# v's last additions by accumulating stores, and the recurrence's late passes placed behind the low parts of weights

## The chip, the cores and the metric

The kernel runs on one core of a Trainium2 chip. The metric is the device time of one execution in microseconds (us); of several executions the median is given. One execution is taken by the hardware profiler, and its trace has the start and the duration of the instructions of each engine: PE (TensorE) with its weight loads, DVE (VectorE), ACT (ScalarE), POOL (GpSimd), and SP, which only issues DMAs.

## The reference, cut to what matters

One layer of a streaming encoder, 512 positions by 1024 channels, in float32. A normalised input h goes through one wide projection; its columns feed a pooling mixer, a gated linear recurrence (RG-LRU), a stick-breaking attention with 8 heads, and three gates. The three branches are merged, projected and added to x, and a gated feed-forward follows. What the change touches:

```
proj = einsum('bsd,dc->bsc', h, w_in)          # q, k, v are 1024 columns each
...
a = exp(log_a);  mult = sqrt(-expm1(2 * log_a));  b = mult * (i * xc)
h_t = a_t * h_{t-1} + b_t                      # the recurrence, a scan over positions
...
out = einsum('bhqk,bkhd->bqhd', w, vb)         # attention reads v
```

## The kernel before, in words

Matrix products run in a split form: a float32 operand is written as a high part (rounded to the type fp32r) plus a low part (the rest), and three matmuls (high-high, high-low, low-high) take the place of one. For weights `split_w` (L134 to L143) does it: ScalarE makes the high part `whi` (L141), VectorE subtracts it for the low part `wlo` (L142). High and low parts have three buffers each, so a part can be made only when TensorE is done with the piece three before. Both are traced with a raised priority; the list `los` keeps the low parts' instructions in order.

v, k and q, in this order (`VKQ`), are computed by a Strassen-like scheme of 7 products in place of 8. The unit's weights are four blocks 11, 12, 21, 22, the inputs are quarters of h and sums of them (T1 to T4). The products come in the order 11, 12, S2, S1, S3, S4, 22 (`ORDER`). Each is cut in two pieces of 12 matmuls, i = 0 and 1; in the texts "12,0" is the first piece of product 12. A unit has 14 pieces, 168 matmuls. The sums of weights are made on the way (`add_seven`, L202 to L225): S1 is 21 + 22 by an accumulating load from POOL's queue (L200), S2 is 21 + 22 + 11 on VectorE (tile `qs`, L214), S3 is 11 + 21 by another accumulating load onto 11 (L215), S4 is 12 + S2 on VectorE (L209). For all units the sum qs and the load of L215 follow directly the split of 11. Three pieces' parts are made ahead of the products (`weights`); at the end of some pieces the loads of the next unit's blocks are issued from SP (L198).

The results accumulate in PSUM, in tiles of 128 x 1024. For each quarter (i, j) of the unit's output, ScalarE copies a snapshot of the accumulator into SBUF (`snap`, L857); some products later `final` (L865) adds the rest, read from PSUM, on VectorE. For v the sum is then stored to DRAM from POOL's queue (`store`, L790), for k and q squares, scaling and a transpose come first. v is read again much later, by the attention.

The recurrence runs beside this, in four chunks of 256 channels (c = 0 to 3): ScalarE makes tanh, exp (L695) and a square root (L698), VectorE two decay passes (`lru_decay`, L703 and L705; for chunks 2 and 3 the second is an affine pass of ScalarE, L707), two input passes (`lru_input`, L711 and L712) and two scans (L717). `lru_store` casts the result on ScalarE (L722), takes the low part on VectorE (L723), and stores both from POOL's queue (L725). These passes are put into a background list (`step`, `bg`) and taken from it, one or two at a time, by `tick` calls between pieces. The late passes of chunks 2 and 3 come while v is computed.

The order of the instructions on each engine is fixed when the program is built, by a planner with its own estimates of time: it takes the ready instruction with the highest priority. `tc.high_priority(n)` raises it. `tc.issue_after(ins)` makes an instruction come not before `ins` on its engine; it doesn't say how soon after. At run time each engine works strictly in its fixed order and waits on semaphores.

Of the kernel before, what the change touches and what calls it, by code (L numbers as in the profile page):

```python
# [64 lines left out]
def layer_kernel(ctx: ExitStack, tc: tile.TileContext, x, xt, vecs, w_in, w_qkv7, w_gate7, w_pool, w_rg, w_ig,  # L65
# [125 lines left out]
    def seven_load(n, nms):  # L191
# [3 lines left out]
        for nm in nms:  # L195
            for i in range(pieces):
                qraw[u, nm, i] = r = b4(list(shape), f"qw{u}{nm}{i}", "w")
                nc.sync.dma_start(r, seven_src(u, nm, i))  # L198
                if nm == "21":
                    nc.gpsimd.dma_start(r, seven_src(u, "22", i), accum_op=ALU.add)  # L200

    def add_seven(un, nm, i):  # L202
        u, pieces, shape = UNITS[un]
        last = i == pieces - 1

        def make(n):
            if nm == "S4":
                r = qraw[u, "12", i]
                dve.tensor_tensor(r, r, qraw[u, "S2", i], ALU.add)  # L209
            src = qraw[u, {"S1": "21", "S3": "11", "S4": "12"}.get(nm, nm), i]  # L210
            parts = split_w(src, [P] + list(shape), n)
            if nm == "11":
                qraw[u, "S2", i] = r = b4(list(shape), f"qs{u}{i}")
                dve.tensor_tensor(r, qraw[u, "21", i], src, ALU.add)  # L214
                add = nc.gpsimd.dma_start(src, seven_src(u, "21", i), accum_op=ALU.add)  # L215
            if last:
                if un < 3:
                    seven_load(un + 1, {"S1": ("21",), "S3": ("11",), "S4": ("12",), "22": ("22",)}.get(nm, ()))
                elif un == 3 and nm == "11":
                    with tc.issue_after(add.ins):  # L220
                        seven_load(un + 1, ("21", "11"))
                elif un == 3:
                    seven_load(un + 1, {"12": ("12",), "S2": ("22",)}.get(nm, ()))
            return parts
        specs.append((("seven", u, nm, i), make))  # L225
# [211 lines left out]
    with ExitStack() as first:  # L437
# [263 lines left out]
        def lru_decay(c):  # L701
            e, t = lru[c]["r"], lru[c]["t"]
            dve.scalar_tensor_tensor(t, e, 1.0, t, ALU.add, ALU.mult)  # L703
            if c < 2:
                dve.tensor_scalar(t, t, -1.0, 1.0, ALU.mult, ALU.add)  # L705
            else:
                act(t, t, AF.Identity, scale=-1.0, bias=1.0)  # L707

# [10 lines left out]
        def lru_store(c):  # L719
            y = lru.pop(c)["i"]  # L720
            h, l = b4([2, S], f"yh{c}", "b", F32R), y.bitcast(F32R)
            act(h, y, AF.Copy)  # L722
            dve.tensor_tensor(l, y, h.bitcast(F32), ALU.subtract)  # L723
# [36 lines left out]
        def of(f, c):  # L760
            return lambda: f(c)
# [17 lines left out]
        gate1(2)  # L779
        for f, c in ((lru_decay, 2), (lru_decay, 3), (lru_input, 2)):  # L780
            step(of(f, c))
# [11 lines left out]
        def post(t, i, j, r):  # L793
            if t == 2:
                store(t, i, j, r)
                return
            z = b4([2, 512], f"sq{t}{i}{j}")
# [51 lines left out]
        for t in VKQ:  # L849
# [4 lines left out]
            def snap(key, src):  # L854
                r[key] = b4([2, 512], f"r{t}{key[0]}{key[1]}")
                with tc.high_priority(EARLY):
                    state["snap"] = act(two(r[key]), in_order(src), AF.Copy, scale=-1.0 if key[0] else 1.0)  # L857

            def post_behind(key):
                with tc.issue_after(state["snap"].ins):  # L860
                    post(t, *key, r[key])

            def final(key, src):
                v = two(r[key])
                dve.tensor_tensor(v, v, in_order(src), ALU.subtract if key[0] else ALU.add)  # L865
# [9 lines left out]
            for nm in ORDER:  # L875
# [19 lines left out]
                else:  # L895
                    final((1, 0), ps["22"])
                if (t, nm) == (VKQ[0], "S3"):
                    def last_scan():
                        for j in range(2):
                            with tc.issue_after(los[j - 5]):  # L900
                                lru_scan(3, j)

                    step(of(lru_input, 3)), step(of(lru_scan, 2)), step(last_scan)
                    step(of(lru_store, 2)), step(of(lru_store, 3))
# [899 lines left out]
```

## Time and profile before

| what | value |
|---|---|
| median of 3 runs | 860.64 us (859.68 to 860.79) |
| the profiled execution's own time | 858.89 us |
| its span, first to last instruction | 856.8 us |
| PE busy | 850.3 us (99%) |
| DVE busy | 732.3 us (85%) |
| ACT busy | 533.3 us (62%) |
| POOL busy | 88.6 us (10%) |
| DMA, mean over the span | 180 GB/s |

Busy times of engines overlap. A matmul of 512 columns shows 0.38 us in its row, but the next one starts 0.216 us after it, since they are pipelined; so a loss of TensorE is read from the distance of starts and not from busy time. In a row of the timeline stand the start, the duration, the engine, the line, the operation, the tile written, the tiles read, their sizes, the count, and in brackets the idle time of the engine just before, with what ended it. In rows of groups, the busy time and the mean duration in ns stand behind the bar.

### The profile page before, as it was taken

To read this page: it belongs to the slowest core of one execution; us is meant where nothing else is said; L and a number is where in the kernel's file an instruction comes from. 1 tells how busy PE (TensorE), PEld (TensorE's weight loads), DVE (VectorE), ACT (ScalarE), POOL (GpSimd) and SP (SyncE) were. 2 spreads that over 40 slices of the span, in tenths; PEclk is the share of its full clock that TensorE was granted. 3 is DMA by queue.
4 is the path that set the end of the run, shared out by engine and by line. 5 is a ranking of instruction groups with operands and counts; after the bars stand their busy time and mean duration, and the time that the engine had idled before them with its cause. 6 is when DMAs were issued, how large, how long until landed. Compare 5 with 4: busy or idle time off the path is not lost.

```text
span 856.8 us, 14307 instructions
## 1 busy us (share of the span) xinstructions
PE 850.3 (99%) x5483; PEld 781.2 (91%) x5483; DVE 732.3 (85%) x937; ACT 533.3 (62%) x863; POOL 88.6 (10%) x128
## 2 busy tenths in 40 slices
PE   9999999999999999999999999999999999999998
PEld 7888888888889988889889988889999999999998
DVE  7899898987897699967997877799988888999974
ACT  6554999658887657556665544455655555755642
POOL 1110002123324102000001100000000000121200
PEclk9999999999999999999999999999999999999999
DMA  9586356798585768846668854364533434797913
GB/s 343 160 286 205 101 167 200 215 316 262 141 257 129 228 170 239 246 116 171 174 204 212 182 197 148 99 164 136 145 99 109 114 101 142 221 238 204 199 32 123
DMA packets 141988, 154.09 MB, mean 180 GB/s; under 512 B 41696, under 2 KB 115424, under 8 KB 141920
## 3 DMA queue, kind: packets, MB, share of 16 engines
q1 hardware_dynamic: 129248, 107.30, 40.6%
q0 software_dynamic: 12528, 45.62, 22.5%
q8 instruction: 43, 0.70, 0.3%
q10 hardware_dynamic: 144, 0.26, 0.1%
q14 instruction: 25, 0.20, 0.1%
HBM read 132.71 MB, written 18.87 MB: 177 GB/s over the span
## 4 chain that ended last, share of the span: by engine, by line
PE 88%; ACT 4%; DVE 4%; issue 3%; POOL 1%; DMA 0%; DVEq 0%; POOLq 0%
PE ps_y L315 11%; PE ps_x L315 8%; PE ps_dy L1723 6%; PE ps_q L844 5%; PE ps_dx L1723 5%; PE ps_br L306 3%; PE ps_br L307 3%; PE ps_br L308 3%; PE ps_bY L1347 3%; PE ps_gy L315 3%; PE ps_gate L736 2%; PE ps_bX L1347 2%; PE ps_gx L315 2%; PE ps_pool L308 2%; PE ps_pool L306 2%
## 5 line engine op out<-in xcount | busy, mean ns | idle before, releaser
L141 ACT ACTIVATE whi<-raw 128x1024 fp32r<-128x1024 f32 x69 | 72.9, 1056 | 75.6 <-PE ps_br L307 18.4
L142 DVE TENSOR_TENSOR wlo<-raw,whi 128x1024 fp32r<-128x1024 f32 x69 | 84.2, 1220 | 22.4 <-ACT whi L141 21.9
L142 DVE TENSOR_TENSOR wlo<-qw,whi 128x1024 fp32r<-128x1024 f32 x48 | 58.3, 1220 | 11.6 <-ACT whi L141 11.2
L141 ACT ACTIVATE whi<-qw 128x1024 fp32r<-128x1024 f32 x48 | 50.4, 1052 | 23.6 <-PE ps_q L844 12.8
L1508 ACT ACTIVATE wh_S<-w_S 128x1024 fp32r<-128x1024 f32 x36 | 38.3, 1063 | 28.7 <-PE ps_y L315 20.0
L1629 POOL DMA_DIRECT2D dw<-in_w_down_dram x20 | 17.0, 855 | 305.3 <-DMA dw<-in_w_down_dram 247.7
L1509 DVE TENSOR_TENSOR wl_S<-w_S,wh_S 128x1024 fp32r<-128x1024 f32 x36 | 43.8, 1220 | 3.3 <-ACT wh_S L1508 3.3
L1508 ACT ACTIVATE wh<-w 128x1024 fp32r<-128x1024 f32 x27 | 28.6, 1061 | 28.0 <-PE ps_x L315 9.4
L1509 DVE TENSOR_TENSOR wl<-w,wh 128x1024 fp32r<-128x1024 f32 x27 | 32.9, 1220 | 8.2 <-ACT wh L1508 8.2
L1508 ACT ACTIVATE whdS<-dw 128x1024 fp32r<-128x1024 f32 x20 | 21.2, 1061 | 20.7 <-PE ps_dy L1723 10.6
L1155 DVE TENSOR_TENSOR_SCAN E<-K,ahead 128x512 f32<-128x512 f32 (+3 forms) x32 | 25.4, 814 | 4.6 <-ACT K L1151 4.6
L1509 DVE TENSOR_TENSOR wldS<-dw,whdS 128x1024 fp32r<-128x1024 f32 x20 | 24.3, 1221 | 5.2 <-ACT whdS L1508 5.2
L306 PE MATMUL ps_lru<-HH,whi 128*128 128x512 f32 x64 | 24.6, 384 | 0.0
L306 PE MATMUL ps_br<-yph,whi 128*128 128x512 f32 x64 | 24.4, 382 | 0.0
L306 PE MATMUL ps_gate<-HH,whi 128*128 128x512 f32 x64 | 24.4, 381 | 0.0
L307 PE MATMUL ps_br<-ypl,whi 128*128 128x512 f32 x64 | 24.3, 380 | 0.0
L306 PE MATMUL ps_pool<-HH,whi 128*128 128x512 f32 x64 | 24.3, 379 | 0.0
L306 PE MATMUL ps_br<-yHH,whi 128*128 128x512 f32 x64 | 24.3, 379 | 0.0
L307 PE MATMUL ps_lru<-HL,whi 128*128 128x512 f32 x64 | 24.3, 379 | 0.0
L308 PE MATMUL ps_lru<-HH,wlo 128*128 128x512 f32 x64 | 24.3, 379 | 0.0
L307 PE MATMUL ps_gate<-HL,whi 128*128 128x512 f32 x64 | 24.3, 379 | 0.0
L308 PE MATMUL ps_gate<-HH,wlo 128*128 128x512 f32 x64 | 24.3, 379 | 0.0
(742 smaller groups left out, 3432.1 us busy)
## 6 DMA issues: line engine op xcount, KB each, us to landing
raw<-in_w_in_dram SPq DMA_DIRECT2D x31, 512.0 KB, 5.1
qw<-in_w_qkv_dram SPq DMA_DIRECT2D x24, 512.0 KB, 7.2
dw<-in_w_down_dram POOLq DMA_DIRECT2D x20, 512.0 KB, 7.7
w<-in_w_ffn_gate_dram SPq DMA_DIRECT2D x36, 256.0 KB, 3.9
w<-in_w_ffn_up_dram SPq DMA_DIRECT2D x36, 256.0 KB, 4.1
raw<-in_w_branch_dram SPq DMA_DIRECT2D x16, 512.0 KB, 3.8
qw<-in_w_qkv_dram POOLq DMA_DIRECT2D x12, 512.0 KB, 7.6
g<-gd SPq DMA_DIRECT2D x24, 256.0 KB, 4.5
```

The costliest lines, as they stand in the source:

```text
L141: act(hi, raw, AF.Copy)
L142: los.append(dve.tensor_tensor(lo, raw, hi.bitcast(F32), ALU.subtract).ins)
L306: nc.tensor.matmul(ps, lh, rh, start=start, stop=False, skip_group_check=skip)
L307: nc.tensor.matmul(ps, lh, rl, start=False, stop=False, skip_group_check=skip)
L308: nc.tensor.matmul(ps, ll, rh, start=False, stop=stop, skip_group_check=skip)
L315: nc.tensor.matmul(o, a_[a][:, w, k, :], il2(b_[b][:, k, :]), start=first and n == k == 0, stop=last and n == 2 and k == 3, skip_group_che ...
L844: nc.tensor.matmul(ps[:, a, :], b_[:, k, ts_], il(a_[:, kk, :]), start=first and n == k == 0, stop=n == 2 and k == 3, skip_group_check=True)
L1155: dve.tensor_tensor_scan(E[:, c0:c0 + n][:, ::-1], K[:, c0 + 1:c0 + n + 1][:, ::-1], ahead[:, S - n:][:, ::-1], 0.0, ALU.mult, ALU.add)
L1347: nc.tensor.matmul(o, ah[x_][:, w, k, :], il2(b[k][y_]), start=first_ and n == k == 0, stop=n == 2 and k == 3, skip_group_check=True)
L1508: act(h, src, AF.Copy)
L1509: dve.tensor_tensor(l, src, h.bitcast(F32), ALU.subtract)
L1723: nc.tensor.matmul(o, a_[a][:, w, k0 + k, :], il2(b_[b][:, k, :]), start=first and i == k == 0, stop=last and i == 2 and k == nk - 1, skip ...
```

## The change

Four things:

1. For v, `final` no longer adds on VectorE. The snapshot is stored to DRAM at once; later ScalarE copies the rest out of PSUM into a new SBUF tile, and an accumulating store from POOL's queue adds it to what is in DRAM (`add_store`).
2. For v's unit (un == 0) the sum qs and the accumulating load onto 11 come after the low part of the same piece of 12 and no longer after 11; the sum S4 comes after the low part of the same piece of S2.
3. The late passes of chunks 2 and 3 leave the background list: lru_input 2 and 3 are placed behind the low parts of 12,0 and 12,1, the scans of chunk 2 behind those of S2,0 and S2,1, the scans of chunk 3 behind those of S1,0 and S1,1. Before, lru_input 2 was a step of its own ahead of v, and lru_input 3 and the scans were steps after v's S3.
4. The second decay pass of chunks 2 and 3 goes from ScalarE to VectorE, and so does the cast in `lru_store` for chunks 0 and 1.

```diff
@@ -199,6 +199,8 @@
                 if nm == "21":
                     nc.gpsimd.dma_start(r, seven_src(u, "22", i), accum_op=ALU.add)
 
+    seven_lo = {}
+
     def add_seven(un, nm, i):
         u, pieces, shape = UNITS[un]
         last = i == pieces - 1
@@ -206,13 +208,18 @@
         def make(n):
             if nm == "S4":
                 r = qraw[u, "12", i]
-                dve.tensor_tensor(r, r, qraw[u, "S2", i], ALU.add)
+                with tc.issue_after(seven_lo["S2", i]) if un == 0 else nullcontext():
+                    dve.tensor_tensor(r, r, qraw[u, "S2", i], ALU.add)
             src = qraw[u, {"S1": "21", "S3": "11", "S4": "12"}.get(nm, nm), i]
             parts = split_w(src, [P] + list(shape), n)
-            if nm == "11":
+            if un == 0:
+                seven_lo[nm, i] = los[-1]
+            if nm == ("12" if un == 0 else "11"):
+                first_ = qraw[u, "11", i]
                 qraw[u, "S2", i] = r = b4(list(shape), f"qs{u}{i}")
-                dve.tensor_tensor(r, qraw[u, "21", i], src, ALU.add)
-                add = nc.gpsimd.dma_start(src, seven_src(u, "21", i), accum_op=ALU.add)
+                with tc.issue_after(los[-1]) if un == 0 else nullcontext():
+                    dve.tensor_tensor(r, qraw[u, "21", i], first_, ALU.add)
+                add = nc.gpsimd.dma_start(first_, seven_src(u, "21", i), accum_op=ALU.add)
             if last:
                 if un < 3:
                     seven_load(un + 1, {"S1": ("21",), "S3": ("11",), "S4": ("12",), "22": ("22",)}.get(nm, ()))
@@ -701,10 +708,7 @@
         def lru_decay(c):
             e, t = lru[c]["r"], lru[c]["t"]
             dve.scalar_tensor_tensor(t, e, 1.0, t, ALU.add, ALU.mult)
-            if c < 2:
-                dve.tensor_scalar(t, t, -1.0, 1.0, ALU.mult, ALU.add)
-            else:
-                act(t, t, AF.Identity, scale=-1.0, bias=1.0)
+            dve.tensor_scalar(t, t, -1.0, 1.0, ALU.mult, ALU.add)
 
         def lru_input(c):
             e, s_ = lru[c]["r"], lru[c]["s"]
@@ -719,7 +723,10 @@
         def lru_store(c):
             y = lru.pop(c)["i"]
             h, l = b4([2, S], f"yh{c}", "b", F32R), y.bitcast(F32R)
-            act(h, y, AF.Copy)
+            if c < 2:
+                dve.tensor_copy(h, y)
+            else:
+                act(h, y, AF.Copy)
             dve.tensor_tensor(l, y, h.bitcast(F32), ALU.subtract)
             for d, t in zip(yd, (h, l)):
                 nc.gpsimd.dma_start(d[c // 2][:, 2 * (c % 2):2 * (c % 2) + 2, :], t)
@@ -777,7 +784,7 @@
         gate1(1)
         step(of(lru_scan, 1)), step(g3, of(lru_store, 0)), step(t3, of(lru_store, 1)), step(of(lru_exp, (2, 3)))
         gate1(2)
-        for f, c in ((lru_decay, 2), (lru_decay, 3), (lru_input, 2)):
+        for f, c in ((lru_decay, 2), (lru_decay, 3)):
             step(of(f, c))
         bg.extend(prepare_t())
         gate1(3)
@@ -791,9 +798,6 @@
 
 
         def post(t, i, j, r):
-            if t == 2:
-                store(t, i, j, r)
-                return
             z = b4([2, 512], f"sq{t}{i}{j}")
             sums = qss[:, 2 * j:2 * j + 2, 4 * i:4 * i + 4] if t == 0 else cst.tile(
                 [P, 2, 4], F32, tag="ssq", name=f"ssq{t}{i}{j}", bufs=2)
@@ -855,12 +859,23 @@
                 r[key] = b4([2, 512], f"r{t}{key[0]}{key[1]}")
                 with tc.high_priority(EARLY):
                     state["snap"] = act(two(r[key]), in_order(src), AF.Copy, scale=-1.0 if key[0] else 1.0)
+                if t == 2:
+                    store(t, *key, r[key])
 
             def post_behind(key):
                 with tc.issue_after(state["snap"].ins):
                     post(t, *key, r[key])
 
+            def add_store(key, src):
+                part = b4([2, 512], f"v{key[0]}{key[1]}")
+                with tc.high_priority(EARLY):
+                    act(two(part), in_order(src), AF.Copy, scale=-1.0 if key[0] else 1.0)
+                nc.gpsimd.dma_start(rows(t, *key), part, accum_op=ALU.add)
+
             def final(key, src):
+                if t == 2:
+                    add_store(key, src)
+                    return
                 v = two(r[key])
                 dve.tensor_tensor(v, v, in_order(src), ALU.subtract if key[0] else ALU.add)
                 if (t, key) == (0, (1, 0)):
@@ -894,13 +909,14 @@
                     final((0, 1), ps["S1"])
                 else:
                     final((1, 0), ps["22"])
+                if t == VKQ[0]:
+                    for f, after_ in {"11": ((lambda: lru_input(2), ("12", 0)), (lambda: lru_input(3), ("12", 1))),
+                                      "12": ((lambda: lru_scan(2, 0), ("S2", 0)), (lambda: lru_scan(2, 1), ("S2", 1))),
+                                      "S2": ((lambda: lru_scan(3, 0), ("S1", 0)), (lambda: lru_scan(3, 1), ("S1", 1)))
+                                      }.get(nm, ()):
+                        with tc.issue_after(seven_lo[after_]):
+                            f()
                 if (t, nm) == (VKQ[0], "S3"):
-                    def last_scan():
-                        for j in range(2):
-                            with tc.issue_after(los[j - 5]):
-                                lru_scan(3, j)
-
-                    step(of(lru_input, 3)), step(of(lru_scan, 2)), step(last_scan)
                     step(of(lru_store, 2)), step(of(lru_store, 3))
 
 
```

## The prediction

> **What bounds the kernel now.** I read the page first: TensorE fills nearly all of the span, and the chain that ended last runs along it.
>
> ```profile
> span 856.8 us, 14307 instructions
> ...
> PE 88%; ACT 4%; DVE 4%; issue 3%; POOL 1%; DMA 0%; DVEq 0%; POOLq 0%
> ```
>
> A matmul that starts late makes the end late; nothing else counts until it reaches TensorE. The profiled execution took 858.89 us, 2.1 us more than its span; the median of the three runs is 860.64 us. I reckon the change in the span and put it on the median.
>
> The change lies in the stretch of v, k and q: three equal units of 7 products, 168 matmuls each (14 pieces of 12). So the next view is TensorE's timeline at the starts of v, k, q and what follows q, with the rows in v that carry a wait.
>
> ```profile
> 138.10 0.38 PE L844 MATMUL ps_q<-whi,HH 128*128 128x512 f32 x1
> ...
> 143.95 0.48 PE L844 MATMUL ps_q<-wlo,HH 128*128 128x512 f32 x1 [0.29 <-DVE wlo L142]
> ...
> 147.35 0.48 PE L844 MATMUL ps_q<-wlo,HH 128*128 128x512 f32 x1 [0.55 <-DVE wlo L142]
> ...
> 160.93 0.48 PE L844 MATMUL ps_q<-wlo,hT3h 128*128 128x512 f32 x1 [0.36 <-DVE wlo L142]
> ...
> 176.36 0.38 PE L844 MATMUL ps_q<-whi,HH 128*128 128x512 f32 x1
> ...
> 212.62 0.38 PE L844 MATMUL ps_q<-whi,HH 128*128 128x512 f32 x1
> ...
> 250.06 0.27 PE L315 MATMUL ps_gy<-HH,whi 128*128 128x256 f32 x1
> ```
>
> The same work takes 38.26 us for v, 36.26 for k and 37.44 for q. k's pace is 36.26/168 = 0.2158 us a matmul, 2.59 a piece. v therefore loses 2.00 us and q 1.18. v's loss is three waits for a low part (wlo) from VectorE, at the second matmul of pieces 12,0, 12,1 and S3,0. That 2.00 us is all that a change inside v can give back.
>
> Why VectorE is late shows in its own timeline:
>
> ```profile
> 136.99 1.23 DVE L703 SCALAR_TENSOR_TENSOR lt<-lr,lt 128x1024 f32<-128x1024 f32 x1 [2.54 <-ACT ls L698]
> 138.13 1.22 DVE L142 TENSOR_TENSOR wlo<-qw,whi 128x1024 fp32r<-128x1024 f32 x1
> 139.27 2.35 DVE L214 TENSOR_TENSOR qs<-qw,qw 128x1024 f32<-128x1024 f32 x2
> 141.54 1.22 DVE L703 SCALAR_TENSOR_TENSOR lt<-lr,lt 128x1024 f32<-128x1024 f32 x1
> 142.68 1.22 DVE L142 TENSOR_TENSOR wlo<-qw,whi 128x1024 fp32r<-128x1024 f32 x1
> 143.81 1.22 DVE L711 SCALAR_TENSOR_TENSOR ls<-lr,ls 128x1024 f32<-128x1024 f32 x1
> 144.95 1.22 DVE L209 TENSOR_TENSOR qw<-qw,qs 128x1024 f32<-128x1024 f32 x1
> 146.08 1.22 DVE L142 TENSOR_TENSOR wlo<-qw,whi 128x1024 fp32r<-128x1024 f32 x1
> ```
>
> From 136.99 on one pass follows another every 1.135 us (142.68 to 146.08 is three steps). A piece lasts 2.59 us, so beside its low part VectorE has room for 1.28 other passes; where two stand between low parts, it falls behind. The low parts at 142.68 and 146.08 end at 143.90 and 147.30, where TensorE restarts 0.05 us later. Ahead of them stand the very passes that the diff moves: qs, the decays, lru_input, the sums S4. The first row also shows VectorE idle for 2.54 us, waiting for ScalarE's square root.
>
> ScalarE's timeline has the rest: the cast that goes to VectorE, the high part of 12,0, and the two affine passes that leave.
>
> ```profile
> 132.15 1.04 ACT L722 ACTIVATE yh<-li 128x1024 fp32r<-128x1024 f32 x1
> ...
> 140.76 1.05 ACT L141 ACTIVATE whi<-qw 128x1024 fp32r<-128x1024 f32 x1
> ...
> 142.27 2.00 ACT L707 ACTIVATE lt<-lt 128x1024 f32<-128x1024 f32 x2
> ```
>
> **The change part by part.** What one pass costs, from the groups of VectorE:
>
> ```profile
> L865 DVE TENSOR_TENSOR r<-r,ps_q 128x1024 f32<-128x1024 f32 x3 | 3.6, 1214 | 0.0
> ...
> L705 DVE TENSOR_SCALAR lt<-lt 128x1024 f32<-128x1024 f32 x2 | 1.4, 688 | 0.0
> ```
>
> *Casts and affine passes.* Two casts (chunks 0 and 1) and two affine passes (chunks 2 and 3) go from ScalarE, about 1.04 us each, to VectorE, 0.69 us each. The casts stand on ScalarE ahead of the square roots for which VectorE idles 2.54 us. Taking them out brings the roots up to 2 x 1.04 = 2.08 us forward, and their 1.38 us on VectorE fits into that idle time. So VectorE gets into v between 0 (if ScalarE finds another wait) and 2 us earlier; I take 1, the middle, since the row shows the wait but not what stands behind it.
>
> *Piece 12,0.* Ahead of its low part the two sums qs leave (2 x 1.135) and two affine passes enter (2 x 0.69): 142.68 - 2.27 + 1.38 = 141.79. The high part ends at 140.76 + 1.05 = 141.81. The low part then ends at 143.03; TensorE wants it at 138.10 + 25 x 0.2158 = 143.50. The first wait goes, with 0.47 us to spare and more if the lead comes.
>
> *Piece 12,1.* It is wanted at 138.10 + 37 x 0.2158 = 146.08. With one pass (its neighbour's sum) behind 12,0's low part it ends at 141.81 + 2 x 1.135 + 1.22 = 145.30; with two passes 146.44, 0.36 late; with three 1.5 late. A lead of 1 us carries two passes. The low parts have higher priority than the recurrence, so I expect one or two.
>
> *Piece S3,0.* Wanted at 138.10 + 97 x 0.2158 = 159.03, so it has to start by 157.81: fourteen steps after 141.81, thirteen passes between. Five low parts and the two sums must come before it; of the other ten (four of lru_input, four scans, two sums S4) six fit, and a seventh with the lead. The two scans of chunk 3 and the sums S4 are wanted by nobody before S3,0, so I take the third wait as gone too.
>
> *v's last additions.* Four passes of 1.21 us leave VectorE, three or four of them inside v. ScalarE gets four copies out of PSUM. No such copy is quoted; the nearest row, its pass of equal size, gives 1.04 us. ScalarE gives up two casts and two affine passes of the same length, so its sum is unchanged. PSUM banks are released by ScalarE instead of VectorE; at k's pace four tiles pass before a bank is wanted again. Below nothing is excluded: nothing here shortens a matmul.
>
> *The added wait.* Each accumulating store has to follow its base store, on POOL's queue; base stores take this long to land:
>
> ```profile
> DMA to landing us min/median/max: 3.7/7.4/10.3
> ```
>
> The last base store (of 1,0) is issued some 2 us after S3 ends (138.10 + 10 x 2.59 + 2 = 166.0) and has landed by 176.3 at the latest; until then POOL may be held. Behind it stand k's two accumulating loads of 11, which k's S3 needs:
>
> ```profile
> L215 POOL DMA_DIRECT2D qw<-in_w_qkv_dram x2: 871/878/884, 174.6 to 178.0; - x2
> DMA to landing us min/median/max: 8.8/9.0/9.1
> ```
>
> Issued at 176.3 and 177.2, the later lands at 186.3. k's S3,0 starts at 176.36 - 2.00 + 8 x 2.59 = 195.1; less the parts' 1.05 + 1.22 us it needs its data at 193. Cost nothing, with over 6 us of cover; each microsecond beyond that would show fully. In a chain it is less: if 1,0's base store is queued behind the hold for 1,1 (base store at 138.10 + 8 x 2.59 + 1.04 = 159.9, landed by 170.2), it lands by 180.5, k's loads by 190.5, and 2.5 us are left.
>
> The Trainium skill, in "DMA: Bandwidth & Descriptors", section "Two DMAs through the same engine are not ordered", says that only the first DMA's completion semaphore orders a second one behind it. By that rule POOL holds at all four, as I have reckoned. If the queue's order were enough, the sum would be the same, and half the chance of the late weights below would go. No row of before has a store that waits for a store.
>
> *Sum.* v falls from 38.26 to 36.26: -2.00 us. Span 854.8, the profiled time 856.9, the median 858.6.
>
> **The rivals.** *Part of the wait stays* (the diff says "not before", and the passes may still be put in pairs). With two passes ahead of 12,1, no lead, and a like slip at S3,0, 0.4 to 1.6 us remain: 859.0 to 860.2, say 859.7. For it: before already has pairs there. Against: the lead, and the additions that leave.
>
> *Slower: VectorE crowded.* Twelve passes other than low parts now follow 12,0's (two qs, two sums S4, four of lru_input, four scans), and there are six gaps between low parts from 12,0 to S3,0. If the order puts two into each, each gap takes 3 x 1.135 = 3.405 us instead of 2.59: 4.9 us behind at S3,0, less 0.5 to 2.5 of slack, is 2.4 to 4.4 us of waiting where 2.00 stood: 861.0 to 863.0, say 862. It decides from more than two gaps with pairs and no lead. Against: each low part outranks the recurrence once its high part is there.
>
> *Slower: k's first weights late.* DMA is full when they come.
>
> ```profile
> 160.00:176.00 16.00, 15.64 (x73) 13.38 (x72) 15.10 (x14) 9.95 (x10) 4.35 (x7) 1.00 0.98 295
> ...
> L198 SPq DMA_DIRECT2D qw<-in_w_qkv_dram x1: 328/328/328, 162.0 to 162.0; - x1
> DMA to landing us min/median/max: 8.7/8.7/8.7
> ```
>
> The DMA share is 0.98 at 295 GB/s, 1.78 us for 512 KB. k's piece 11,1 landed at 170.7; by the rows above it is wanted at 176.36 - 2.00 + 13 x 0.2158 - 2.27 = 174.9, 4.2 us later. If two base stores that used to come later and three accumulating ones all fall ahead of it, it is 8.9 late: 4.7 us of waiting, 863.3. POOL's holds in a chain reach the same loads' partners at S3, with 2.5 us of cover less these delays. Against: the loads are issued when v's parts of 11 are made, which come earlier too. I give the transfers 0.03 and the chain of holds 0.03.
>
> *More than v.* q's 1.18 us go as well, if k's lighter VectorE lets q's passes run ahead: 857.5.
>
> **How the numbers follow.** All of v's loss goes: 0.45, at 858.6. Part stays: 0.27. VectorE crowded: 0.13. Weights late: 0.06. q too: 0.09. The measurement of this kernel can tell about 0.2%, 1.72 us, from no change: faster means below 858.92. The likeliest case lies only 0.3 below that, and the three runs of before lie 1.1 us apart; two thirds of it count as faster, which with the q case gives 0.40. Slower, above 862.36, takes half of the crowded case and most of the late weights: 0.12. The rest, 0.48, is within. The range goes from the q case less a little, 857.3, to the middle of the crowded case, 862.0; outside are its upper half, the late weights and a little below, under 0.2. The likeliest case's own range is 857.9 to 859.4.
>
> **What would show it.** v from its first matmul to k's first: 36.3 us if right, 37 to 38 if part stays, above 38.3 if crowded. No wait for wlo at 12,0; the square roots about 2 us earlier against v's start; decays wholly on VectorE. A wait of TensorE or of a high part at k's first pieces would mean the late weights, one at k's S3 POOL's hold. I am wrong in kind if v keeps its 38.26 with the same three waits, or if time changes outside 138 to 250 us.

## The result, and the profile after

The kernel after takes 861.88 us (median of 22 executions, 857.66 to 865.46), the kernel before 859.30 us in the same series (22 executions, 858.16 to 860.98; the 860.64 us above were three). The recorded ratio of the two sets is 1.0024, 95% interval 1.0015 to 1.0034 (that of the medians is 1.0030): slower by some 0.2 to 0.3%, where the forecast was 2.00 us less, 858.6 us counted from the 860.64. The spread has grown as well, from 2.8 to 7.8 us. The profiled execution of after took 860.44 us, 1.4 us less than its median, so it shows the smaller part of the loss.

The page of the profile, after: the span, and the shares of the chain that ended last.

```profile
span 858.7 us, 14319 instructions
...
PE 83%; DVE 6%; ACT 5%; issue 3%; DMA 3%; POOL 1%; SPq 0%; POOLq 0%; DVEq 0%; ACTq 0%
```

TensorE's share of the chain has fallen from 88% to 83%, and DMA, which had 0%, has 3%: a hint that work now waits for a transfer, and no more (e14's chain, below, has 4% without the waits that follow). TensorE's timeline of after says where: the first matmuls of v, k, q and of what follows, and the late ones between.

```profile
137.65 0.38 PE L848 MATMUL ps_q<-whi,HH 128*128 128x512 f32 x1
...
159.49 0.48 PE L848 MATMUL ps_q<-wlo,hT3h 128*128 128x512 f32 x1 [0.53 <-DVE wlo L142]
...
162.86 0.48 PE L848 MATMUL ps_q<-wlo,hT3h 128*128 128x512 f32 x1 [0.51 <-DVE wlo L142]
...
175.69 0.38 PE L848 MATMUL ps_q<-whi,HH 128*128 128x512 f32 x1
...
210.21 0.48 PE L848 MATMUL ps_q<-wlo,hT4h 128*128 128x512 f32 x1 [0.46 <-DVE wlo L142]
...
212.69 0.38 PE L848 MATMUL ps_q<-whi,HH 128*128 128x512 f32 x1
...
224.78 0.48 PE L848 MATMUL ps_q<-wlo,hT2h 128*128 128x512 f32 x1 [0.75 <-DVE wlo L142]
...
251.25 0.27 PE L322 MATMUL ps_gy<-HH,whi 128*128 128x256 f32 x1
```

And the matmul of before at the same place in q's S2,0:

```profile
223.66 0.48 PE L844 MATMUL ps_q<-wlo,hT2h 128*128 128x512 f32 x1 [0.29 <-DVE wlo L142]
```

v takes 38.04 us (38.26 before), k 37.00 (36.26), q 38.56 (37.44). The waits at 12,0 and 12,1 are gone; two stand at S3,0 and S3,1; a new one is in k's last piece, and the one at q's S2,0 has grown from 0.29 to 0.75 us. Against before the span grows by 1.9 us: -0.45 ahead of v, -0.22 in v, +0.74 in k, +1.12 in q, +0.67 behind q. That last term lies between 0.0 and 1.5 in this profile and in all those below but one, whatever was edited (6.4 in e10's, with waits at 350 and 784 us), so no cause is sought for it.

What k and q wait for begins on POOL. Its timeline in after (L797 is a base store, L873 an accumulating store, L222 k's accumulating load onto 11):

```profile
162.78 1.04 POOL L797 DMA_DIRECT2D qd<-r  x1
174.73 1.21 POOL L873 DMA_DIRECT2D qd<-v  x1 [10.91 <-ACT whi L141]
175.47 1.22 POOL L797 DMA_DIRECT2D qd<-r  x1
...
177.84 2.31 POOL L222 DMA_DIRECT2D qw<-in_w_qkv_dram  x2
...
180.84 1.20 POOL L873 DMA_DIRECT2D qd<-v  x1
182.37 1.20 POOL L873 DMA_DIRECT2D qd<-v  x1 [0.33 <-ACT r L861]
```

POOL stands idle for 10.91 us between a base store and its accumulating store. ScalarE's name in that row can't be the reason, since its copy of that tile (L872, at 166.50) was done 7 us earlier; with another target, in e5 below, POOL waits only for that copy. So it is the hold for the landing of the base store. Such a hold is what the rule of the Trainium skill that the prediction weighed asks for ("DMA: Bandwidth & Descriptors", "Two DMAs through the same engine are not ordered"); no run here shows whether the queue's order alone would have been enough. With the held store, ten transfers of 512 KB leave within 8 us. The busy share of the DMA engines from 176 to 200 us, in 40 slices, first before and then after:

```profile
DMA  9999999999999999999994028770598138999937
```

```profile
DMA  9989999999999999999999999999999999999999
```

Before, the queues run empty at about 189 us; after, they don't. The loads of q's blocks are issued at that time. The next fence has landing times in after: the four accumulating stores, and the two accumulating loads from POOL that make q's sum 21 + 22 (L200).

```profile
L873 POOL DMA_DIRECT2D qd<-v x4: 1199/1204/1207, 153.1 to 182.4; - x4
...
DMA to landing us min/median/max: 5.8/12.8/21.6
```

```profile
L200 POOL DMA_DIRECT2D qw<-in_w_qkv_dram x2: 865/892/918, 196.8 to 199.4; - x2
DMA to landing us min/median/max: 11.0/11.6/12.2
```

L200's two loads took 5.6 and 8.6 us before. They also leave about 3 us later than before (196.75 and 199.37, against 193.8 and 196.1), since each adds onto the plain load of the same block, and both plain loads (issued at 188.6 and 191.3) now take 7.5 us to land in place of 3.5. VectorE's timeline of after shows who waits:

```profile
202.94 1.22 DVE L142 TENSOR_TENSOR wlo<-qw,whi 128x1024 fp32r<-128x1024 f32 x1
207.79 1.23 DVE L221 TENSOR_TENSOR qs<-qw,qw 128x1024 f32<-128x1024 f32 x1 [3.64 <-DMA qw<-in_w_qkv_dram]
208.93 1.22 DVE L142 TENSOR_TENSOR wlo<-qw,whi 128x1024 fp32r<-128x1024 f32 x1
```

VectorE works in its fixed order: q's first sum qs waits 3.64 us for its transfer, and k's last low part stands behind it. That low part ends at 210.15, and TensorE restarts at 210.21. Before, the same sum started at 204.74 without a wait.

q's loss follows from the same late sum. VectorE's timeline of after, and then ScalarE's:

```profile
215.97 1.21 DVE L880 TENSOR_TENSOR r<-r,ps_q 128x1024 f32<-128x1024 f32 x1
217.10 1.22 DVE L142 TENSOR_TENSOR wlo<-qw,whi 128x1024 fp32r<-128x1024 f32 x1
```

```profile
217.34 0.31 ACT L807 ACTIVATE sq<-r 128x128 f32<-128x128 f32 x1 [1.63 <-DVE r L880]
```

VectorE is now behind: the low part of q's 12,0 ends at 218.32, and its matmul starts at 218.37, 0.50 us after the one before it. k's last addition (L880) comes 1.14 us later than before, ScalarE waits for it, and the high part of S2,0, behind ScalarE's squares and scalings, starts at 222.43 in place of 221.29.

### The profile page after: what moved, and what is told of

It is laid out like the page before. It is cut to its first block, busy times and chain, and to the rows that moved or that the text cites. A ratio compares the mean times of both kernels' runs of the same rounds, so it can differ in the third digit from the quotient of the medians.

```text
span 858.7 us, 14319 instructions
## 1 busy us (share of the span) xinstructions
PE 850.6 (99%) x5483; PEld 782.0 (91%) x5483; DVE 730.5 (85%) x937; ACT 532.4 (62%) x863; POOL 92.5 (11%) x132
## 3 DMA queue, kind: packets, MB, share of 16 engines
q0 software_dynamic: 13616, 47.72, 23.9%
## 4 chain that ended last, share of the span: by engine, by line
PE 83%; DVE 6%; ACT 5%; issue 3%; DMA 3%; POOL 1%; SPq 0%; POOLq 0%; DVEq 0%; ACTq 0%
PE ps_y L322 11%; PE ps_x L322 8%; PE ps_dy L1739 6%; PE ps_dx L1739 5%; PE ps_br L315 3%; PE ps_br L313 3%; PE ps_br L314 3%; PE ps_q L848 3%; PE ps_gy L322 2%; PE ps_gate L743 2%; DMA qw<-in_w_qkv_dram 2%; DVE wlo L142 2%; PE ps_gx L322 2%; PE ps_bY L1363 2%; PE ps_pool L315 2%
## 5 line engine op out<-in xcount | busy, mean ns | idle before, releaser
L315 PE MATMUL ps_br<-yHH,wlo 128*128 128x512 f32 x64 | 24.3, 380 | 0.0
L314 PE MATMUL ps_pool<-HL,whi 128*128 128x512 f32 x64 | 24.3, 380 | 0.0
L314 PE MATMUL ps_br<-yHL,whi 128*128 128x512 f32 x64 | 24.3, 380 | 0.0
```

Source lines behind the costliest of these rows:

```text
L314: nc.tensor.matmul(ps, lh, rl, start=False, stop=False, skip_group_check=skip)
L315: nc.tensor.matmul(ps, ll, rh, start=False, stop=stop, skip_group_check=skip)
```

## The experiments

Theory A: the accumulating stores fill the DMA queues, and q's loads come late; POOL's hold makes it worse. Rivals: B, the new places of passes on VectorE cost the time; C, the hold alone does. In the table stand the units of each profile in us, the median of 5 to 12 executions (after: 22), and the ratio to before in the same series, with its 95% interval.

| kernel | v | k | q | v+k+q | median | ratio |
|---|---|---|---|---|---|---|
| before | 38.26 | 36.26 | 37.44 | 111.96 | 859.30 | 1 |
| after | 38.04 | 37.00 | 38.56 | 113.60 | 861.88 | 1.0024 (1.0015 to 1.0034) |
| e1_no_add | 37.73 | 36.26 | 37.53 | 111.52 | 858.46 | 0.9984 (0.9976 to 0.9993) |
| e2_add_only | 37.64 | 42.51 | 36.92 | 117.07 | 864.75 | 1.0055 (1.0043 to 1.0067) |
| e4_plain_over | 38.05 | 36.26 | 37.55 | 111.86 | 858.53 | 0.9988 (0.9980 to 0.9997) |
| e5_add_apart | 38.05 | 36.89 | 38.48 | 113.42 | 860.08 | 1.0002 (0.9991 to 1.0013) |
| e6_scans_spread | 36.63 | 36.93 | 38.00 | 111.56 | 858.62 | 0.9992 (0.9984 to 1.0001) |
| e7_q_sum_behind | 38.05 | 36.26 | 39.07 | 113.38 | 861.08 | 1.0025 (1.0013 to 1.0036) |
| e8_no_add_no_cast | 39.15 | 36.26 | 37.54 | 112.95 | 859.90 | 1.0007 (0.9999 to 1.0016) |
| e10_one_add | 38.06 | 36.26 | 37.43 | 111.75 | 859.20 | 1.0006 (0.9993 to 1.0019) |
| e11_plain_twice | 38.05 | 37.41 | 38.44 | 113.90 | 861.16 | 1.0019 (1.0007 to 1.0032) |
| e12_add_late11 | 39.92 | 37.32 | 37.36 | 114.60 | 863.31 | 1.0049 (1.0033 to 1.0065) |
| e13_add_rows | 38.04 | 36.73 | 36.88 | 111.65 | 858.19 | 0.9987 (0.9978 to 0.9996) |
| e14_add_rows_v | 38.05 | 36.26 | 37.11 | 111.42 | 859.50 | 1.0008 (0.9995 to 1.0020) |

**Undo the accumulating stores (e1), or make nothing else of the change (e2).** In e1, parts 2 to 4 of the change stay:

```diff
         def post(t, i, j, r):
+            if t == 2:
+                store(t, i, j, r)
+                return
...
-                if t == 2:
-                    store(t, *key, r[key])
...
-                if t == 2:
-                    add_store(key, src)
-                    return
```

> The change with v's last additions back on VectorE (no accumulating stores); order of the recurrence and of the sums, casts and affine passes as changed. Theory (the stores fill DMA, q's loads land late, and q's sum holds VectorE's queue): 857.5 to 859 us, runs within 2 us of each other, no idle time of VectorE on q's sum qs, q's two accumulating loads landed by 206 us. Rival (the order on VectorE costs the time): about 861.5, as the change.

e2 is the kernel before with these lines of the change put in.

> The kernel before with the accumulating stores alone. Theory of the stores: 861 to 863 us, runs spread over 5 us or more. Rival (order on VectorE): 858.5 to 859.5, like before or a little faster, spread as before.

e1 is faster than before and the best complete kernel here; e2 is 5.4 us slower, more than expected, and its spread is 1.8 us where 5 were expected. So part 1 alone turns the change's sign, and B falls for the sum of it. TensorE's timeline of e2:

```profile
177.23 0.48 PE L841 MATMUL ps_q<-wlo,HH 128*128 128x512 f32 x1 [1.52 <-DVE wlo L142]
...
213.68 0.48 PE L841 MATMUL ps_q<-wlo,hT4h 128*128 128x512 f32 x1 [2.51 <-DVE wlo L142]
214.00 0.58 PE L841 MATMUL ps_q<-whi,hT4l 128*128 128x512 f32 x1
214.38 0.63 PE L841 MATMUL ps_q<-whi,hT4h 128*128 128x512 f32 x1
214.80 0.63 PE L841 MATMUL ps_q<-wlo,hT4h 128*128 128x512 f32 x1
...
217.36 0.43 PE L841 MATMUL ps_q<-wlo,hT4h 128*128 128x512 f32 x1
217.63 0.38 PE L841 MATMUL ps_q<-whi,hT4l 128*128 128x512 f32 x1
```

The second wait is at the same place as in after, and five times as long. The first, in k's 11,0, lies one piece ahead of the place that the prediction's rival of late weights had named; in after it isn't there. It isn't the load of 11,1 either: k's second sum qs, ahead of that low part on VectorE, waits 2.29 us for k's own load from L200. After the second stall the matmuls start 0.42 us apart, twice the usual distance, until 217.36.

**Plain stores in their place (e4), and another target (e5).** e4 keeps every instruction, its order and the hold, but doesn't add:

```diff
-                nc.gpsimd.dma_start(rows(t, *key), part, accum_op=ALU.add)
+                nc.gpsimd.dma_start(rows(t, *key), part)
```

> The change with the second store of each quarter of v plain in place of accumulating: same bytes from SBUF, same place, same wait for the base store, order of all engines the same; v lacks its base part. If the accumulation itself loads DMA: 858 to 859.5 and small spread. If POOL's hold for the base store, which bunches what is queued behind, makes the lateness: as the change, about 861.5. If four more transfers of 512 KB do it: the same 861.5. If VectorE's order does it: 861.5.

e5 adds, but into DRAM that nothing else touches, so that no store waits for a store:

```diff
-                nc.gpsimd.dma_start(rows(t, *key), part, accum_op=ALU.add)
+                nc.gpsimd.dma_start(qx[key[0]][key[1] * H:(key[1] + 1) * H, :].rearrange("(a p) c -> p a c", p=P), part, accum_op=ALU.add)
```

> The change with the accumulating stores into another DRAM buffer: no wait for the base store, accumulation and bytes kept, order of all engines the same; v lacks its last additions. If POOL's hold makes the lateness: 858 to 859.5 and small spread. If the accumulation or the bytes do it: 861 to 862.5 and spread over 5 us or more. If VectorE's order does it: 861.5.

With plain stores k and q are as before, though POOL waits 12.20 us ahead of the second of them: C falls, and four more plain transfers of 512 KB cost nothing. With accumulation and no hold q and k are as late as in after in the profile; the median lies 1.6 us above e4's on the same chip (the two intervals just overlap), between the two forecasts. After, with both, lies 1.8 us above e5, but comes from another series, and their profiles are nearly alike (113.60 against 113.42): that the hold makes accumulation worse is likely, not shown.

**Transfer time alone (e11).** e4, and each of its four stores made a second time:

```diff
                 nc.gpsimd.dma_start(rows(t, *key), part)
+                nc.gpsimd.dma_start(qx[key[0]][key[1] * H:(key[1] + 1) * H, :].rearrange("(a p) c -> p a c", p=P), part)
```

> The change with v's four last additions stored plainly over the base parts (their sums are left out of v), and each of the four stored a second time, plainly, into DRAM that nothing reads. Eight plain transfers of 512 KB at about 1.8 us of all 16 DMA engines are 14.4 us, against some 12 us for the four accumulating ones of the change, in the same places of the same queue, with the hold of POOL kept. Theory that DMA time in the full stretch is what k and q lose: k 37 us, q 38.5 us, a median of 861 to 863. Rival, that accumulating costs by its kind (reading back, order of its packets) and not by the time it fills: like the plain stores alone, k 36.3, q 37.5, 858.5 (857.9 to 859.3).

VectorE's timeline of e11, where q's sum waits:

```profile
208.87 1.22 DVE L221 TENSOR_TENSOR qs<-qw,qw 128x1024 f32<-128x1024 f32 x1 [4.06 <-issue]
```

Plain stores, if there are enough of them, do the same: L200's loads land in 11.0 to 12.4 us, the sum starts 1.1 us later than in after, and the time is 861.16. So it doesn't take accumulation to lose this time; what it adds to a plain store may be no more than the room that it takes. The wait of this sum goes with what k takes: none in before (start 204.74, k 36.26), 0.41 us in e4 (205.18, 36.26), 3.54 in e5 (208.04, 36.89), 3.64 in after (207.79, 37.00), 4.06 in e11 (208.87, 37.41). With a start up to about 206, as in e4, e13 and e14, it doesn't reach TensorE.

**Longer rows (e13, e14).** The software queue has 12528 packets in before, 13104 in e4 and 13616 in after: 272 packets for an accumulating store, 144 for a plain one of the same size. e13 is e5 with each partition's two rows of 2 KB side by side:

```diff
-... .rearrange("(a p) c -> p a c", p=P), part, accum_op=ALU.add)
+... .rearrange("(p a) c -> p a c", p=P), part, accum_op=ALU.add)
```

> The accumulating stores into separate DRAM (no hold, v's last additions left out), with the target's rows laid out so that each partition writes 4 KB in a row in place of two rows of 2 KB. Theory that the number of packets makes an accumulating store dear: the software queue's packets fall from 13616 to about 13104, each store costs near the plain 1.8 us, k 36.3, q 37.5, median 858.5 (857.9 to 859.2). Rival, that each byte accumulated is dear whatever the packets: the queue's share stays at 23.8%, k 36.9, q 38.5, 860.1 (859.6 to 860.7).

The issue and landing times of e5's accumulating stores, and then of e13's:

```profile
L874 POOL DMA_DIRECT2D qx<-v x4: 1199/1204/1207, 150.9 to 184.3; - x4
...
DMA to landing us min/median/max: 6.0/15.4/19.9
```

```profile
L874 POOL DMA_DIRECT2D qx<-v x4: 855/862/871, 150.5 to 183.2; - x4
...
DMA to landing us min/median/max: 6.3/14.3/17.2
```

The packets fell to 13104, as expected, and the median to 858.19, 1.9 us below e5 (another chip). L200's loads land in 7.6 to 8.6 us in place of 10.0 to 11.3, and the sum qs starts at 205.79. But the queue's share of the 16 engines stayed at 23.9%, which the rival had expected, and k doesn't recover fully (36.73): its own second sum waits 0.97 us for a load from L200, and the low part of 11,0, behind that sum, comes late. The intervals of e5 and e13 overlap a little (0.9991 to 0.9996), so the case for the row length rests on the profiles, in which the late wait in k's last piece is gone with nothing else edited; why the loads beside the stores land sooner at an equal share is open.

e14 is the whole change with v kept in that order in DRAM; the attention reads it back in two loads a head:

```diff
-            return qd[t, i][j * H:(j + 1) * H, :].rearrange("(a p) c -> p a c", p=P)
+            return qd[t, i][j * H:(j + 1) * H, :].rearrange("(p a) c -> p a c" if t == 2 else "(a p) c -> p a c", p=P)
...
-                            nc.sync.dma_start(r, qd[t, g][:, hd].rearrange("(b p) c -> p b c", p=P))
+                            for jj in range(2):
+                                nc.sync.dma_start(r[:, 2 * jj:2 * jj + 2, :], qd[t, g][jj * H:(jj + 1) * H, hd].rearrange("(p a) c -> p a c", p=P))
```

> The whole change, with v kept in DRAM in another order of rows: each partition's two rows of 2 KB lie side by side, so that base and accumulating stores write 4 KB in one piece; the attention reads v back with two loads of 256 KB a head in place of one of 512 KB. POOL's hold for the base stores stays, and so do the sums. Theory that the two short rows make the accumulating stores dear and that the hold alone costs nothing: v 38.05, k 36.3 to 36.9, q 36.9 to 37.6, median 858.2 to 859.6, the sixteen extra loads in the attention costing nothing or up to 0.5. Rival, that hold and accumulation together fill the queue at k whatever the length of a row (the queue's share was 23.9% with long rows too): waits near 210, 219 and 225 us as in the change, k 37, q 38.5, median 860.5 to 862.

VectorE's timeline of e14 at the same place:

```profile
206.19 1.22 DVE L221 TENSOR_TENSOR qs<-qw,qw 128x1024 f32<-128x1024 f32 x1 [1.41 <-DMA qw<-in_w_qkv_dram]
```

k takes 36.26 us and q 37.11, with POOL's hold of 10.63 us still there: in this profile the added waits in k and q are gone. The median, 859.50, is 2.4 us below after's, from another series. It is no gain over before: three of the twelve executions took 862.3 to 863.3, so a slip is still near.

**One early addition (e10), the last two late (e12).** e10 adds by a store only for (0,0), at 153 us, ahead of the crowd; the other three are added on VectorE:

```diff
-                if t == 2:
+                if t == 2 and key == (0, 0):
```

> The change with the accumulating store for quarter 0,0 alone, the other three added on VectorE. If three late accumulating stores into a full DMA queue are the loss: as without the stores, 858.2 to 858.8, small spread. Rival (each accumulating store costs its share, wherever it falls): 859.3, a quarter of the 3.4 us between the change and the change without stores.

One accumulating store leaves 12800 packets. The stretch is as clean as before, 111.75, in a profile of the slowest execution (864.25), which loses its time behind q. But the median, 859.20, is what the rival forecast (859.3) and not the theory (858.2 to 858.8); the interval holds 1 and touches e1's. So one early store doesn't cost what four do, and whether it costs nothing isn't shown. e12 issues the stores of (0,1) and (1,0) behind q's own loads onto 11:

```diff
-NAW, NAT, NAB = 8, 8, 13
+NAW, NAT, NAB = 8, 8, 11
...
+            if last and (un, nm) == (2, "11"):
+                with tc.issue_after(add.ins):
+                    while behind:
+                        behind.pop(0)()
```

> The change with v's last two additions, (0,1) and (1,0), issued behind q's own loads onto 11, at about 216 us, where the DMA queues are nearly empty (share 0.2 from 220 to 230); their two tiles are taken out of the 13 rotating buffers, which leaves 11. The first two additions stay where they are. Theory that accumulating stores cost time only where they stand in the full queue of 175 to 205 us: k 36.3 to 36.6, q 37.5 to 37.8, median 858.6 to 859.6. Rival, that an accumulating store is dear wherever it stands, or that POOL's hold of 11 us for the second addition is what makes k and q late: k 36.9, q 38.5, 861 or more. If 11 buffers are too few, waits of ScalarE or VectorE for a buffer show outside the low parts.

TensorE's timeline of e12:

```profile
144.51 0.48 PE L853 MATMUL ps_q<-wlo,HH 128*128 128x512 f32 x1 [0.78 <-DVE wlo L142]
...
178.90 0.48 PE L853 MATMUL ps_q<-wlo,HH 128*128 128x512 f32 x1 [0.80 <-DVE wlo L142]
```

q is back at 37.36 and k's last piece has no wait, as theory A says; but eleven buffers bring the waits of v back (39.92 us) and a new one into k's 11,0, and the time is the worst but one. Inconclusive: two things were changed at once.

**Move q's sum (e7).** In after, k's last low part stands behind q's sum. e7 puts that sum behind the low part of 12, as v has it:

```diff
-            if nm == ("12" if un == 0 else "11"):
+            if nm == ("12" if un in (0, 2) else "11"):
...
-                with tc.issue_after(los[-1]) if un == 0 else nullcontext():
+                with tc.issue_after(los[-1]) if un in (0, 2) else nullcontext():
```

> The change with q's two sums qs (and the load behind them) put behind q's low parts of 12, as v's are. If the late loads reach TensorE because q's sum stands in VectorE's queue ahead of k's last low parts: k back at 36.3 to 36.5 us, median 859 to 860 and less spread. Rival (the loads reach TensorE through q's own weights, wherever the sum stands): 861 to 862.5 and spread as in the change.

k recovers fully (36.26), as the theory has it: its loss comes from the sum's place on VectorE. But q loses more (39.07), and the median is the rival's, though not by the rival's way. VectorE's timeline of e7 in q:

```profile
229.54 0.17 DVE L350 TENSOR_TENSOR krs<-rsqq 128x8 f32<-128x8 f32 x1 [1.45 <-POOL rsqq L349]
```

The moved sums run at 216.41 and 219.81 without waiting for a transfer. TensorE is late at S1,0 (0.44 us) and S3,0 (0.78), and the low part of S1,0 comes at 230.23 behind another chain: VectorE's sums of squares (225.48), POOL's product on them (L349, 225.83), and the scale of the row above. Why this chain runs so late in e7 isn't traced further, and that q needs the late weights itself isn't shown.

**Spread the scans (e6), undo the casts (e8).** Both start from e1. e6 places the scans behind the low parts of S3 and S4:

```diff
-"12": ((lambda: lru_scan(2, 0), ("S2", 0)), (lambda: lru_scan(2, 1), ("S2", 1))),
-"S2": ((lambda: lru_scan(3, 0), ("S1", 0)), (lambda: lru_scan(3, 1), ("S1", 1)))
+"S1": ((lambda: lru_scan(2, 0), ("S3", 0)), (lambda: lru_scan(2, 1), ("S3", 1))),
+"S3": ((lambda: lru_scan(3, 0), ("S4", 0)), (lambda: lru_scan(3, 1), ("S4", 1)))
```

> The change without its accumulating stores, and the four scans one by one behind the low parts of S3,0, S3,1, S4,0 and S4,1 in place of S2 and S1. If pairs of passes between two low parts cost the 1.0 us of waits that are left in v without the stores: v in 36.3 to 36.8 us (37.73 with the scans in pairs), median 857.0 to 857.8. Rival (those waits come from VectorE's total work, not from the pairs): v stays near 37.7 with the waits later on, median 858.5.

VectorE's timelines ahead of S3 show what made v's two waits, first in after and then in e6:

```profile
154.84 1.21 DVE L142 TENSOR_TENSOR wlo<-qw,whi 128x1024 fp32r<-128x1024 f32 x1
155.96 1.23 DVE L716 TENSOR_TENSOR ls<-ls,li 128x1024 f32<-128x1024 f32 x1
157.09 1.23 DVE L721 TENSOR_TENSOR_SCAN li<-lt,ls 128x512 f32<-128x512 f32 x1
158.23 1.21 DVE L142 TENSOR_TENSOR wlo<-qw,whi 128x1024 fp32r<-128x1024 f32 x1
159.34 2.34 DVE L721 TENSOR_TENSOR_SCAN li<-lt,ls 128x512 f32<-128x512 f32 x2
```

```profile
157.76 1.22 DVE L142 TENSOR_TENSOR wlo<-qw,whi 128x1024 fp32r<-128x1024 f32 x1
158.89 1.22 DVE L721 TENSOR_TENSOR_SCAN li<-lt,ls 128x512 f32<-128x512 f32 x1
160.03 1.20 DVE L142 TENSOR_TENSOR wlo<-qw,whi 128x1024 fp32r<-128x1024 f32 x1
161.15 1.22 DVE L721 TENSOR_TENSOR_SCAN li<-lt,ls 128x512 f32<-128x512 f32 x1
```

In after two passes stand between low parts, and S3,0's low part ends at 159.44, 0.05 us ahead of the late matmul; in e6 one does, and v falls to 36.63, 0.37 above k's pace. The median doesn't follow (858.62, against 858.46 for e1 on another chip): k and q take 0.67 and 0.47 us more than in e1. The traces show where the gain went: counted from v's first matmul, VectorE's later passes come at the same time in both (the low part of k's 11,1 starts 38.56 us behind it in e6 and 38.55 in e1, k's addition ahead of q's S2,0 76.33 and 76.30), and TensorE, further ahead in e6, waits for them in k and q. For the three units together that agrees with the rival, VectorE's total work. In e8 the two casts and the two affine passes are back on ScalarE:

```diff
-            dve.tensor_scalar(t, t, -1.0, 1.0, ALU.mult, ALU.add)
+            if c < 2:
+                dve.tensor_scalar(t, t, -1.0, 1.0, ALU.mult, ALU.add)
+            else:
+                act(t, t, AF.Identity, scale=-1.0, bias=1.0)
...
-            if c < 2:
-                dve.tensor_copy(h, y)
-            else:
-                act(h, y, AF.Copy)
+            act(h, y, AF.Copy)
```

> The change without its accumulating stores and with the two casts and two affine passes back on ScalarE: only the places of the sums and of the recurrence's late passes are left. If the casts give VectorE the lead into v: square roots end about 2 us later against v's start than without the stores alone, a wait at 12,0 or 12,1 of 0.3 us or more, median 858.8 to 859.5. Rival (the places alone do it): median 858.5, no wait at 12.

VectorE's timeline of e8 has the old wait for the square root again:

```profile
136.39 1.23 DVE L710 SCALAR_TENSOR_TENSOR lt<-lr,lt 128x1024 f32<-128x1024 f32 x1 [2.54 <-ACT ls L705]
```

v is 1.42 us longer than in e1, with waits at 12,1 (0.40 us) and S2,0 (1.68), and the median 1.4 us, on another chip (2.0 by the two ratios). What e1 gains over before thus needs the move of the casts and affine passes: without it the new places of the sums and the late passes give nothing. The move with the old places wasn't run.

## Why the prediction was wrong

**Casts and affine passes: right, and sized too low.** The rows of after, ScalarE's and then VectorE's:

```profile
133.57 2.01 ACT L705 ACTIVATE ls<-lt 128x1024 f32<-128x1024 f32 x2
```

```profile
134.66 2.36 DVE L710 SCALAR_TENSOR_TENSOR lt<-lr,lt 128x1024 f32<-128x1024 f32 x2 [0.72 <-ACT ls L705]
...
140.08 1.23 DVE L142 TENSOR_TENSOR wlo<-qw,whi 128x1024 fp32r<-128x1024 f32 x1 [0.72 <-ACT whi L141]
...
143.49 1.22 DVE L142 TENSOR_TENSOR wlo<-qw,whi 128x1024 fp32r<-128x1024 f32 x1
```

The decays start at 134.66 in place of 136.99; v starts 0.45 us earlier too, so VectorE's lead is 1.88 us, where 0 to 2 was given and 1 taken. It is worth 1.4 us by e8 against e1, with the new places around it.

**Pieces 12,0 and 12,1: right.** Their low parts end at 141.31 and 144.71 (forecast 143.03 and 145.30), and both waits are gone.

**Piece S3,0: wrong.** It was to be gone because the scans of chunk 3 and the sums S4 "are wanted by nobody before S3,0". A pass doesn't come late because nobody wants it: between the low parts of 12,0 and S3,0 eight of the ten optional passes ran (both sums S4, the four of lru_input, both scans of chunk 2), where six or seven fit, and the two scans of chunk 3 came right behind, ahead of S3,1. The case "part of the wait stays" (0.27) was the true one for v; it left 1.8 us of the 2.00, more than its 0.4 to 1.6. Of the 3.9 us between the span's forecast (-2.0) and its change (+1.9) this is 1.8; k and q are 1.9, and the rest lies ahead of v (-0.45) and behind q (+0.67).

**The added wait: "Cost nothing, with over 6 us of cover". This is the step that failed.** The hold came in the form that the prediction calls a chain, and longer: for the base store of (1,1) POOL was held until 174.7 (forecast 170.2), and the base store of (1,0) stood behind it. k's loads left by 178.4 and landed by 192.4 (14.0 us in place of 9.1; forecast 190.5); the cover was nearly used up, but k's S3 doesn't wait, so the hold by itself cost nothing, as e4 shows too. Ahead of (0,0)'s store POOL stood idle for 5.33 us, ahead of the last two for at most 0.33. What the step left out is that the stores, once they go, are transfers among others. The prediction asked who stands behind them on POOL's queue, and not who shares the DMA engines with them in the following 25 us: q's loads. A store's 512 KB was priced as any 512 KB, 1.78 us; by the queue's share (23.9% against 22.6% in e1, of 857 us, over four stores) an accumulating one takes some 2.8 us of all 16 engines, an estimate with the rounding of the shares in it (and e13, with the same share, loses less). What it cost is the 3.4 us between e1 and after. e4 shows that at the plain price the step would have held, e11 that twice as many plain transfers undo it.

**Late weights, at 0.06: the right kind, in another place.** The rival had the full queue, but looked only at k's 11,1, where before the change the row of a late load stood nearest; in after TensorE is late 35 us further on. Its 863.3 was worked out for that piece, which isn't late in after, so that the result came near it (861.88) is no support. With the price of an accumulating store unknown and no row for it, the cover should have been worked out for every load of the following unit, and this chance been larger.

**VectorE crowded, at 0.13: near in number by luck.** Its 861.0 to 863.0 holds the result, and the stated range reached it by this case. But its sign, v above 38.3 us, isn't there: v takes 38.04, and the time is lost in k and q.

**v's last additions: right as far as they go.** In e4, which has ScalarE's four copies, TensorE waits for nothing but low parts. But v isn't shorter for it either: 38.05 us, against 37.73 in e1, where VectorE still adds.

## What to carry to other kernels

A transfer that nobody waits for still takes room: where the queues run empty only just before the next weights are issued, work out the landing of each later load with the new bytes ahead of it, not only what waits behind the instruction. Price an accumulating store by its rows, and lay the target out so that a partition writes one long row. Where moves are bundled, test each alone: here the gain was gone without one of them (two casts and two affine passes, 1.4 us), and another (the stores, 3.4 us) lost more than that.

## What the runs showed of the hardware

- An accumulating store of 512 KB in rows of 2 KB makes 272 packets and takes 1.20 us to issue on POOL; in rows of 4 KB it makes 144 and takes 0.86 us. A plain store in rows of 2 KB makes 144 and takes 0.74 us in before (v's base stores in after: 1.04 to 1.22 us).
- The software queue's packets put the kernels with v's stores at their early places in order: 13616 and 13680 (after, e5, e7, e11, e2) go with late loads for q, 13104 and less (e4, e13, e14, e10) don't. The queue's share of time doesn't (23.8 to 24.0% in after, e5, e7, e11, and in e13 and e14). That packets are the cause is not shown by this.
- Beside the stores with shorter rows the loads of L200 landed later (10.0 to 12.2 us in e5 and after, against 7.4 to 8.7 in e13 and e14), though the queue's share of the engines is the same.
- In e2, after a wait of 2.51 us, matmuls of 512 columns started 0.42 us apart for 3.4 us (214.00 to 217.36), and the slice from 210 to 220 us has a granted clock (the third number from the right) of 0.83:

```profile
210.00:220.00 10.00, 7.49 (x27) 5.91 (x26) 8.13 (x12) 4.34 (x18) 3.63 (x4) 0.83 0.93 283
```

The wait thus costs more than its own length; the stalls of 0.5 to 0.8 us in after show no such drop (its clock is 1.00 throughout the stretch). The Trainium skill, "TensorE: Matmul & The Clock Gate", section "Part 1: The HAM clock gate (the "warmup" mystery)", says that the clock halves after an idle window of about 3.4 us and comes back after a busy one of the same length. The halving and the 3.4 us agree; the idle time that was enough here is shorter, 2.51 us.
